# Layer norm sums of a four-layer transformer block: values and squares side by side in one TensorE matmul

## The chip, the cores and the metric

The kernel runs on one core of one Trainium2 chip. The metric is the device time of one execution in microseconds (us); the number given for a kernel is the median of several executions. The engines are named as in the profile: PE is TensorE (PEld its weight loads), DVE is VectorE, ACT is ScalarE, POOL is GpSimd, SP is SyncE, whose queue issues the DMAs.

## The reference

Four layers work on 256 latent tokens and 256 context tokens of 1024 features. Each layer is a token mixer (three kinds of attention) and a gated feed-forward network (FFN), and each of the two is followed by a layer norm. In the last layer only the latent tokens are carried on. What matters here is the norm:

```python
def layer_norm(t, g, b):
    tf = t.astype(jnp.float32)
    mu = jnp.mean(tf, axis=-1, keepdims=True)
    var = jnp.mean(jnp.square(tf - mu), axis=-1, keepdims=True)
    y = (tf - mu) * lax.rsqrt(var + LN_EPS)
    return (y * g + b).astype(t.dtype)
...
x = layer_norm(DEEPNORM_ALPHA * x + g1 * y, ln_g[i, 0], ln_b[i, 0])
f = swiglu(modulate(x, sh2, sc2), w_ffn_gate[i], w_ffn_up[i], w_ffn_down[i])
x = layer_norm(DEEPNORM_ALPHA * x + g2 * f, ln_g[i, 1], ln_b[i, 1])
```

The same two lines hold for the context tokens in layers 0 to 2. That makes 3 x 4 + 2 = 14 norms of 256 tokens each.

## The kernel before

**Layout.** Activations lie with features on the 128 partitions and tokens along the free axis. The residual stream is eight tiles `X[c]`, c = 0 to 7 (a "chunk" of 128 features each), 128 x 512 in fp32; columns 0 to 255 are the latent tokens (stream 0), 256 to 511 the context tokens (stream 1). Large products are three fp32r matmuls each (high x high, high x low, low x high), so every weight tile is loaded (`raw`), rounded by ACT (`whi`) and its rest taken by DVE or POOL (`wlo`).

**The order of work.** The kernel doesn't issue instructions as it goes. It notes them in a `Planner`, which knows the dependences and a cost for every instruction, makes 16 list schedules, keeps the one with the shortest modelled span and issues in that order. So each engine has one fixed queue, and any edit that changes a cost, a dependence or a number of buffers gives a new order everywhere. The planner's charge for a plain fp32 matmul goes by its columns: 0.083 us up to 64 columns, 0.06 us up to 128 (method `cost`). All noted instructions have the one source line L165, so the profile is read by tile names.

**The norm.** `close()` runs the last projection before a norm: for each chunk a group of matmuls (`half`, or both streams together), then `resid` (DVE adds the PSUM tile to the chunk: "DVE x") and `Norm.add(c)`. With two streams, stream 1 gets its last four chunks first, so that its norm runs while PE still has stream 0 to do; the norm of stream 0 runs under the next projections. In the last layer there is one stream, and after the last chunk PE has nothing else to do until the norm is through.

`Norm.add(c)` has ACT square the chunk (`sq`, four buffers). Chunks 0 to 6 are summed by POOL, values into `zs` and squares into the first `sq` tile, two adds of 128 x 256 for each chunk from 1 on: 12 in a norm. Chunk 7 isn't added by POOL; `REST = 1` is the number of such chunks.

`Norm.sums()` sums over the partitions by matmul with a 128 x 32 tile `ones` (filled with 1/1024). The 256 tokens go to four column groups of the array, 64 tokens each (j = 0 to 3), so that the result lies in PSUM as four blocks of 32 partitions with the means in columns 0 to 63 and the mean squares in columns 64 to 127. There are four groups of four matmuls, each matmul of 64 columns: POOL's `zs`, then chunk 7 itself (`x`), then POOL's `sq`, then chunk 7's `sq`. In the profile a plain fp32 matmul stands as two records, so one group is x8. Then follow, one behind the other, ACT and DVE instructions on 128 x 64 tiles (`v`, `R`, `Rh`, `Rl`), the matmuls with `sel` that spread the result over all partitions (`spread`, in the last norm `spread_apart`), and `apply`, two DVE instructions for each chunk, with ACT and POOL making the next `hh` and `hl`.

**The ring.** Most activation tiles come from one ring of `NSLOT = 46` slots of 2 KB per partition (tag "act"); the planner hands a slot on when the last use of its tile has ended. Some DMAs load into this ring (`rawa` in layer 0, `bias` in layer 1).

Of the kernel before, what the change touches and what calls it, by code (L numbers as in the profile page):

```python
# [12 lines left out]
F32 = mybir.dt.float32  # L13
F32R = mybir.dt.float32r
BF16 = mybir.dt.bfloat16
AF = mybir.ActivationFunctionType
# [3 lines left out]
P = 128  # L20
D = 1024
DC = D // P
T = 512
NL = 256
DEPTH = 4
# [5 lines left out]
END = (0, 1, 2, 3)  # L31
AHEAD = 0
REST = 1
NSLOT = 46
NPAIR = 6
NRAW = 4
LOOK = 2
# [4 lines left out]
LAT = slice(0, NL)  # L42
CTX = slice(NL, T)
SS = (LAT, CTX)
# [367 lines left out]
def block_kernel(ctx: ExitStack, tc: tile.TileContext, a: dict, out: bass.AP):  # L412
    nc = tc.nc
# [28 lines left out]
    nc = plan  # L442
# [65 lines left out]
            loaded[0] += 1  # L508
        return ahead.pop(key)

    X = [const.tile([P, T], F32, name=f"x{c}") for c in range(DC)]
    lng = const.tile([P, DEPTH, 2, DC], F32, name="lng")
    lnb = const.tile([P, DEPTH, 2, DC], F32, name="lnb")
    gq = const.tile([P, 3], F32, name="gq")
# [69 lines left out]

    def mod_split(hh, hl, c, s, S, B, lo_eng):
        ts = SS[s]
        xc = X[c][:, ts]
        h32 = sm.tile([P, NL], F32, tag="h32", name="h32", bufs=4)
        nc.scalar.activation(hh[c][:, ts], xc, AF.Identity, bias=B, scale=S)
        if c % 2 == 0:  # L590
            nc.scalar.activation(h32, xc, AF.Identity, bias=B, scale=S)
        else:
            nc.vector.tensor_scalar(h32, xc, S, B, op0=ALU.mult, op1=ALU.add)
        lo_eng.tensor_sub(hl[c][:, ts], h32, f(hh[c][:, ts]))
# [6 lines left out]
    class Norm:  # L601


        def __init__(self, s, l, k):
            self.s, self.n, self.zl, self.ql = s, 0, [], []
            self.g, self.b = lng[:, l, k], lnb[:, l, k]
            self.v = sm.tile([P, 3, 64], F32, tag="v", name="v", bufs=3)
            nc.scalar.activation(self.v[:, 2, 0:1], latest[0], AF.Sqrt, scale=0.0)

        def add(self, c):  # L610
            z = X[c][:, SS[self.s]]
            sq = sm.tile([P, NL], F32, tag="sq", name="sq", bufs=4)
            nc.scalar.activation(sq, z, AF.Square)
            self.n += 1
            if self.n == 1:
                self.z, self.q = z, sq
            elif self.n == 2:
                z2 = sm.tile([P, NL], F32, tag="zs", name="zs", bufs=3)
                nc.gpsimd.tensor_add(z2, self.z, z)
                nc.gpsimd.tensor_add(sq, self.q, sq)  # L620
                self.z, self.q = z2, sq
            elif self.n <= DC - REST:
                nc.gpsimd.tensor_add(self.z, self.z, z)
                nc.gpsimd.tensor_add(self.q, self.q, sq)
            else:
                self.zl.append(z)
                self.ql.append(sq)

        def sums(self):
            ps = psum("tp")  # L630
            for k, ts in enumerate(([self.z] + self.zl, [self.q] + self.ql)):
                for i, t in enumerate(ts):
                    for j in range(4):
                        nc.tensor.matmul(ps[32 * j:32 * j + 32, 64 * k:64 * k + 64], ones, t[:, 64 * j:64 * j + 64],
                                         start=i == 0, stop=i == REST)
            R = sm.tile([P, 2, 64], F32, tag="R", name="R", bufs=2)
            v = self.v
            nc.scalar.activation(v[:, 0], ps[:, 0:64], AF.Square)
            nc.vector.tensor_sub(v[:, 1], ps[:, 64:128], v[:, 0])
            nc.vector.tensor_scalar(v[:, 1], v[:, 1], 0.0, LN_EPS / ALPHA ** 2, op0=ALU.max, op1=ALU.add)  # L640
            nc.scalar.activation(v[:, 2], v[:, 1], AF.Sqrt)
            nc.vector.reciprocal(R[:, 0], v[:, 2])
            nc.vector.tensor_mul(R[:, 1], ps[:, 0:64], R[:, 0])
            rh = sm.tile([P, 2, 64], F32R, tag="Rh", name="Rh", bufs=2)
            self.R = sm.tile([P, 2, 64], F32R, tag="Rl", name="Rl", bufs=2)
            nc.vector.tensor_copy(rh, R)
            nc.vector.scalar_tensor_tensor(self.R, f(rh), neg, R, op0=ALU.mult, op1=ALU.add)
# [12 lines left out]

        def apply(self, c, h=None):
            s = self.s
            z = X[c][:, SS[s]]
            nc.vector.tensor_mul(z, z, self.bc[:, 0])
            nc.vector.tensor_sub(z, z, self.bc[:, 1])
            if h is not None:
                hh, hl, S, B = h
                mod_split(hh, hl, c, s, S[:, c, s:s + 1], B[:, c, s:s + 1], nc.gpsimd)

        def affine(self, c):  # L670
            z = X[c][:, SS[self.s]]
            nc.scalar.activation(z, z, AF.Identity, scale=self.g[:, c:c + 1], bias=self.b[:, c:c + 1])

        def steps(self, h, norms):
# [10 lines left out]
            return [self.sums, self.spread] + [lambda c=c: two(c) for c in range(0, DC, 2)]  # L685

    def resid(ps, c, s, G):
        z = X[c][:, SS[s]]
        nc.vector.scalar_tensor_tensor(z, ps, G[:, c, s:s + 1], z, op0=ALU.mult, op1=ALU.add)

    def close(load, mm, G, norms, streams, h):
# [760 lines left out]
    def begin(q):  # L1452
        c0 = 2 * q
        for c in (c0, c0 + 1):
            nc.sync.dma_start(X[c], a["x"][:, c, :])
        yield from ada_first(m, q)
        nc.vector.tensor_scalar(S0[:, c0:c0 + 2, :], m[:, 8 + c0:10 + c0, :], 1.0, None, op0=ALU.add)
        for c in (c0, c0 + 1):
# [10 lines left out]
    for l in range(DEPTH):  # L1469
# [26 lines left out]
        if last:  # L1496
# [4 lines left out]
            norms[0].spread_apart()  # L1501
            fin = norms[0]
            for c in range(DC):
                z = X[c][:, LAT]
                w = sm.tile([P, NL], F32, tag="h32", name="h32", bufs=4)
                nc.scalar.activation(w, fin.bc[1][:, :NL], AF.Identity, scale=ng[:, c:c + 1], bias=fin.b[:, c:c + 1])
                nc.vector.scalar_tensor_tensor(z, z, fin.g[:, c:c + 1], fin.bc[0][:, :NL], op0=ALU.mult, op1=ALU.mult)
# [117 lines left out]
```

## Time and profile before

| | |
|---|---|
| median of 3 executions | 2066.43 us (2065.88 to 2066.45) |
| the profiled execution, its own time | 2066.53 us |
| span of that execution in the trace | 2064.7 us |
| PE busy | 2027.8 us (98% of the span) |
| DVE, ACT, POOL busy | 1477.5, 955.9, 416.4 us (72%, 46%, 20%) |
| mean granted TensorE clock | 0.993 |

The span runs from the first to the last instruction that the profile shows; the profiled execution took 1.8 us more than its span. PE is busy nearly all the time, so a change counts where PE does less, or where PE waits for something. The profile has one row for instructions of one kind that follow each other; times are us from the start of the span, "idle before" names what ended the engine's wait.

### The profile page before, as it was taken

Reading aid. Unit: us, or ns where it says so; the run is one execution under the profiler, and the core shown is the slowest. Engines: PE = TensorE matmul, PEld = TensorE weight load, DVE = VectorE, ACT = ScalarE, POOL = GpSimd, SP = SyncE. Lnnn points to the kernel's source line nnn. Section 1 sums busy time; section 2 is a strip of 40 time slices with the busy share of each in tenths; the row PEclk is TensorE's granted clock in tenths of the full one; section 3 lists DMA queues with packets and bytes.
Section 4 is the critical chain, followed back from the end, with each engine's and each line's share of the span. In section 5 each row is a group of like instructions: output and inputs, shape, how many; then the busy total and the mean of one; then the engine's idle time right before and its main releaser. Section 6 shows DMA issues by size and latency. Waiting matters only on the chain.

```text
span 2064.7 us, 31918 instructions
## 1 busy us (share of the span) xinstructions
PE 2027.8 (98%) x12048; PEld 1758.4 (85%) x12048; DVE 1477.5 (72%) x2549; ACT 955.9 (46%) x1684; POOL 416.4 (20%) x508
## 2 busy tenths in 40 slices
PE   8999999999999999999999999999999999989997
PEld 5779988888898888988888898898888888789997
DVE  4797978796487776888785376668877845985564
ACT  4564622223387674722222386745222234766443
POOL 0345200000343334300000342251000005441002
PEclk9999999999999999999999999999999999999998
DMA  9524466665222212466564131126555642234552
GB/s 362 196 67 143 162 196 214 192 216 173 88 85 85 82 62 93 149 198 203 173 203 156 55 103 52 42 83 197 192 197 180 203 132 74 93 123 144 186 192 72
DMA packets 92120, 300.17 MB, mean 145 GB/s; under 512 B 11328, under 2 KB 11456, under 8 KB 91968
## 3 DMA queue, kind: packets, MB, share of 16 engines
q1 hardware_dynamic: 91968, 298.14, 44.5%
q8 instruction: 95, 1.56, 0.3%
q14 instruction: 57, 0.47, 0.1%
HBM read 297.05 MB, written 1.05 MB: 144 GB/s over the span
## 4 chain that ended last, share of the span: by engine, by line
PE 91%; DVE 4%; ACT 2%; issue 1%; DMA 1%; POOL 0%; SPq 0%; DVEq 0%; ACTq 0%; POOLq 0%
PE ps L165 91%; DVE wlo L165 1%; DVE nm L165 1%; ACT stk L165 1%; DVE stl L165 1%; DVE x L165 0%; ACT p L165 0%; DVE ptl L165 0%; ACT whi L165 0%; DMA bada<-in_b_ada 0%; DMA rawa<-in_w_ada 0%; DVE ps L165 0%; DVE stk L165 0%; POOL sq L165 0%; ACT x L165 0%
## 5 line engine op out<-in xcount | busy, mean ns | idle before, releaser
L165 ACT ACTIVATE whi<-raw 128x1024 fp32r<-128x1024 f32 (+3 forms) x371 | 380.1, 1028 | 757.9 <-PE ps L165 441.5
L165 PE MATMUL ps<-hh,whi 128*128 128x512 f32 (+1 forms) x1648 | 578.8, 354 | 1.7 <-ACT hh L165 1.7
L165 PE MATMUL ps<-hh,wlo 128*128 128x512 f32 (+1 forms) x1648 | 580.3, 353 | 0.0
L165 PE MATMUL ps<-hl,whi 128*128 128x512 f32 (+1 forms) x1648 | 579.9, 353 | 0.3 <-POOL hl L165 0.3
L165 DVE TENSOR_TENSOR wlo<-raw,whi 128x1024 fp32r<-128x1024 f32 (+3 forms) x359 | 439.5, 1227 | 119.2 <-ACT whi L165 117.4
L165 DVE SCALAR_TENSOR_TENSOR junk<-raw,sil 128x1024 bf16<-128x1024 f32 x320 | 392.4, 1226 | 101.3 <-DMA raw<-in_w_ada 98.6
L165 PEld LDWEIGHTS ps<-hh,wlo 128*128 128x128 f32 x1648 | 312.3, 190 | 42.2
L165 PEld LDWEIGHTS ps<-hl,whi 128*128 128x128 f32 x1648 | 312.4, 190 | 41.5 <-POOL hl L165 0.5
L165 PEld LDWEIGHTS ps<-hh,whi 128*128 128x128 f32 x1648 | 310.9, 190 | 42.1 <-ACT hh L165 1.9
L165 PE MATMUL ps<-gh,wlo 128*128 128x512 f32 (+1 forms) x800 | 271.9, 341 | 0.0
L165 PE MATMUL ps<-gh,whi 128*128 128x512 f32 (+1 forms) x800 | 271.5, 340 | 0.0
L165 PE MATMUL ps<-gl,whi 128*128 128x512 f32 (+1 forms) x800 | 271.5, 340 | 0.0
L165 DVE SCALAR_TENSOR_TENSOR x<-ps,G,x 128x256 f32<-128x256 f32 x224 | 101.8, 479 | 118.7 <-PE ps L165 118.5
L165 POOL TENSOR_TENSOR zs<-x,x 128x256 f32<-128x256 f32 x14 | 14.0, 1001 | 846.0 <-DVE x L165 846.0
L165 PEld LDWEIGHTS ps<-gl,whi 128*128 128x128 f32 x800 | 151.5, 190 | 17.1
L165 PEld LDWEIGHTS ps<-gh,wlo 128*128 128x128 f32 x800 | 151.5, 190 | 17.0
L165 PEld LDWEIGHTS ps<-gh,whi 128*128 128x128 f32 x800 | 151.6, 190 | 16.9
L165 POOL TENSOR_SCALAR p<-p,r 128x512 f32<-128x512 f32 (+1 forms) x144 | 98.9, 693 | 253.2 <-DVE r L165 232.7
L165 PE MATMUL ps<-whi,hh 128*128 128x512 f32 (+3 forms) x352 | 122.7, 350 | 1.8 <-ACT hh L165 1.8
L165 PE MATMUL ps<-wlo,hh 128*128 128x512 f32 (+3 forms) x352 | 120.7, 344 | 0.0
L165 PE MATMUL ps<-whi,hl 128*128 128x512 f32 (+3 forms) x352 | 117.8, 343 | 0.0
L165 PE MATMUL ps<-oh,wlo 128*128 128x256 f32 (+1 forms) x352 | 109.3, 316 | 0.0
(205 smaller groups left out, 3089.3 us busy)
## 6 DMA issues: line engine op xcount, KB each, us to landing
raw<-in_w_gu SPq DMA_DIRECT2D x176, 512.0 KB, 4.1
raw<-in_w_ada SPq DMA_DIRECT2D x160, 512.0 KB, 4.0
raw<-in_w_d SPq DMA_DIRECT2D x64, 448.0 KB, 4.0
rawa<-in_w_ada SPq DMA_DIRECT2D x64, 256.0 KB, 5.6
raw<-in_w_d SPq DMA_DIRECT2D x32, 512.0 KB, 3.6
raw<-in_a_qkv SPq DMA_DIRECT2D x24, 512.0 KB, 4.4
raw<-in_a_wo SPq DMA_DIRECT2D x16, 512.0 KB, 3.5
raw<-in_b_qk SPq DMA_DIRECT2D x16, 512.0 KB, 3.3
```

Of the source, the lines that this page charges most:

```text
L165: op.fn = lambda: getattr(getattr(self.nc, queue), method)(*p, **k)
```

## The change

In `sums()` the values and the squares of a group are now one moving operand of 2 x 64 columns. For this they must lie in one tile: the running sums in a new tile `zq` (128 x 2 x 256, two buffers, in place of `zs`), chunk 7 and its square in a new constant tile `end` (both streams, 128 x 2 x 2 x 256), of which the values' half takes the place of `X[7]` in all code (`xs(c, s)`). The two groups `zq` and `end` are four matmuls of 128 columns each: 8 matmuls of 128 columns where 16 of 64 columns stood. In the last layer one chunk more isn't added by POOL (`rest` is 2 there): chunk 6 and its square go to the array as two groups of 64 columns between the other two, and 10 POOL adds stand where 12 stood. The sums, squares and everything behind `sums()` are as before. The ring has 45 slots.

```diff
-NSLOT = 46
+NSLOT = 45
...
-    X = [const.tile([P, T], F32, name=f"x{c}") for c in range(DC)]
+    X = [const.tile([P, T], F32, name=f"x{c}") for c in range(DC - 1)]
+    end = const.tile([P, 2, 2, NL], F32, name="end")
+
+    def xs(c, s):
+
+        return X[c][:, SS[s]] if c < DC - 1 else end[:, s, 0]
...
         def __init__(self, s, l, k):
-            self.s, self.n, self.zl, self.ql = s, 0, [], []
+            self.s, self.rest, self.single = s, REST + (l == DEPTH - 1), []
...
         def add(self, c):
-            z = X[c][:, SS[self.s]]
+            z = xs(c, self.s)
+            if c == DC - 1:
+                nc.scalar.activation(end[:, self.s, 1], z, AF.Square)
+                return
+            if c == 0:
+                self.zq = sm.tile([P, 2, NL], F32, tag="zq", name="zq", bufs=2)
+                nc.scalar.activation(self.zq[:, 1], z, AF.Square)
+                return
             sq = sm.tile([P, NL], F32, tag="sq", name="sq", bufs=4)
             nc.scalar.activation(sq, z, AF.Square)
-            self.n += 1
-            if self.n == 1:
-                self.z, self.q = z, sq
-            elif self.n == 2:
-                z2 = sm.tile([P, NL], F32, tag="zs", name="zs", bufs=3)
-                nc.gpsimd.tensor_add(z2, self.z, z)
-                nc.gpsimd.tensor_add(sq, self.q, sq)
-                self.z, self.q = z2, sq
-            elif self.n <= DC - REST:
-                nc.gpsimd.tensor_add(self.z, self.z, z)
-                nc.gpsimd.tensor_add(self.q, self.q, sq)
-            else:
-                self.zl.append(z)
-                self.ql.append(sq)
+            if c >= DC - self.rest:
+                self.single.append((z, sq))
+                return
+            nc.gpsimd.tensor_add(self.zq[:, 0], xs(0, self.s) if c == 1 else self.zq[:, 0], z)
+            nc.gpsimd.tensor_add(self.zq[:, 1], self.zq[:, 1], sq)
 
         def sums(self):
             ps = psum("tp")
-            for k, ts in enumerate(([self.z] + self.zl, [self.q] + self.ql)):
-                for i, t in enumerate(ts):
-                    for j in range(4):
-                        nc.tensor.matmul(ps[32 * j:32 * j + 32, 64 * k:64 * k + 64], ones, t[:, 64 * j:64 * j + 64],
-                                         start=i == 0, stop=i == REST)
+            both = [self.zq, end[:, self.s]]
+            for i, t in enumerate(both):
+                if i == 1:
+                    for k, x in [(k, x) for zq in self.single for k, x in enumerate(zq)]:
+                        for j in range(4):
+                            nc.tensor.matmul(ps[32 * j:32 * j + 32, 64 * k:64 * k + 64], ones, x[:, 64 * j:64 * j + 64],
+                                             start=False, stop=False)
+                for j in range(4):
+                    nc.tensor.matmul(ps[32 * j:32 * j + 32, 0:P].rearrange("p (k t) -> p k t", k=2), ones,
+                                     t[:, :, 64 * j:64 * j + 64], start=i == 0, stop=i == 1)
...
-            nc.sync.dma_start(X[c], a["x"][:, c, :])
+            nc.sync.dma_start(X[c] if c < DC - 1 else end[:, :, 0], a["x"][:, c, :])
```

All other lines of the diff put `xs(c, s)` where `X[c][:, SS[s]]` stood.

## Rows read from the trace of the kernel before

**Rows 1.** The page's part 1, TensorE: busy us, share, instructions
```profile
PE 2027.8 (98%) x12048; PEld 1758.4 (85%) x12048; DVE 1477.5 (72%) x2549; ACT 955.9 (46%) x1684; POOL 416.4 (20%) x508
```
**Rows 2.** PE's waits, 20 to 1790 us, first and last of nine: us, times, longest
```profile
PE ps L165 <- ACT p L165: 1.7, 5, 0.5
...
PE ps L165 <- ACT oh L165: 0.2, 1, 0.2
```
**Rows 3.** Timeline of PE, a norm of layer 0: start us, us, instruction xrecords
```profile
560.93 0.28 PE L165 MATMUL ps<-gl,whi 128*128 128x256 f32 x1
...
561.39 0.41 PE L165 MATMUL ps<-sq,ones 128*32 128x64 f32 x16
...
561.95 0.28 PE L165 MATMUL ps<-gh,whi 128*128 128x256 f32 x1
562.07 0.28 PE L165 MATMUL ps<-gl,whi 128*128 128x256 f32 x1
```
**Rows 4.** Timeline of PE, the first norm, whose sums stand in two blocks
```profile
196.27 0.28 PE L165 MATMUL ps<-ol,whi 128*128 128x256 f32 x1
196.48 0.32 PE L165 MATMUL ps<-zs,ones 128*32 128x64 f32 x8
...
197.06 0.28 PE L165 MATMUL ps<-oh,whi 128*128 128x256 f32 x1
...
197.75 0.43 PE L165 MATMUL ps<-sq,ones 128*32 128x64 f32 x16
```
**Rows 5.** Timeline of PE, layer 0: 32-column weights, 128 moving columns, two blocks
```profile
23.74 0.64 PE L165 MATMUL ps<-rawa,condp 128*32 128x128 f32 x16
...
30.93 0.86 PE L165 MATMUL ps<-rawa,condp 128*32 128x128 f32 x24
```
**Rows 6.** Timeline of POOL, first norm of the last layer
```profile
1845.09 0.74 POOL L165 TENSOR_TENSOR zs<-zs,x 128x256 f32<-128x256 f32 x1 [3.34 <-DVE x L165]
...
1848.19 1.71 POOL L165 TENSOR_TENSOR sq<-sq 128x256 f32<-128x256 f32 x1
...
1850.55 1.70 POOL L165 TENSOR_TENSOR sq<-sq 128x256 f32<-128x256 f32 x1
```
**Rows 7.** Timeline of PE, the same norm
```profile
1849.42 0.28 PE L165 MATMUL ps<-oh,wlo 128*128 128x256 f32 x1
1850.64 0.32 PE L165 MATMUL ps<-zs,ones 128*32 128x64 f32 x8 [0.94 <-POOL zs L165]
...
1852.31 0.43 PE L165 MATMUL ps<-sq,ones 128*32 128x64 f32 x16 [1.23 <-POOL sq L165]
```
**Rows 8.** Timeline of ACT, the same norm
```profile
1849.80 0.94 ACT L165 ACTIVATE sq<-x 128x256 f32<-128x256 f32 x2 [0.44 <-DVE x L165]
1850.64 1.04 ACT L165 ACTIVATE whi<-raw 128x1024 fp32r<-128x1024 f32 x1
1852.80 0.22 ACT L165 ACTIVATE v<-ps 128x64 f32<-128x64 f32 x1 [1.12 <-PE ps L165]
```
**Rows 9.** Timeline of DVE, the same norm
```profile
1850.14 3.19 DVE L165 TENSOR_TENSOR wlo<-raw,whi 128x1024 fp32r<-128x1024 f32 x2
1853.26 0.21 DVE L165 TENSOR_TENSOR v<-ps,v 128x64 f32<-128x64 f32 x1
```
**Rows 10.** Stretches behind this norm: busy us by engine, PEclk (granted clock), DMA
```profile
1858.50:1862.50 4.00, 4.00 (x18) 3.95 (x19) 3.93 (x12) 3.63 (x8) 3.10 (x5) 0.50 0.01 4
1863.00:1867.00 4.00, 4.00 (x35) 4.00 (x34) 1.17 (x4) 2.58 (x5) 2.41 (x4) 1.00 0.00 0
```
**Rows 11.** Timeline of all engines, the last norm of the program
```profile
2050.92 0.73 POOL L165 TENSOR_TENSOR sq<-sq 128x256 f32<-128x256 f32 x1
...
2051.38 0.42 ACT L165 ACTIVATE sq<-x 128x256 f32<-128x256 f32 x1 [0.78 <-DVE x L165]
...
2051.70 0.46 PE L165 MATMUL ps<-sq,ones 128*32 128x64 f32 x16
```
**Rows 12.** PE's waits in the whole span, DMA alone: us, times, longest
```profile
PE ps L165 <- DMA rawa<-in_w_ada: 6.5, 5, 4.0
```

More of the change, by code (lines that the diff above doesn't have):

```diff
@@ L586, in mod_split @@
         ts = SS[s]
-        xc = X[c][:, ts]
+        xc = xs(c, s)
         h32 = sm.tile([P, NL], F32, tag="h32", name="h32", bufs=4)
@@ L662, in apply @@
             s = self.s
-            z = X[c][:, SS[s]]
+            z = xs(c, s)
             nc.vector.tensor_mul(z, z, self.bc[:, 0])
@@ L670, in affine @@
         def affine(self, c):
-            z = X[c][:, SS[self.s]]
+            z = xs(c, self.s)
             nc.scalar.activation(z, z, AF.Identity, scale=self.g[:, c:c + 1], bias=self.b[:, c:c + 1])
@@ L687, in resid @@
     def resid(ps, c, s, G):
-        z = X[c][:, SS[s]]
+        z = xs(c, s)
         nc.vector.scalar_tensor_tensor(z, ps, G[:, c, s:s + 1], z, op0=ALU.mult, op1=ALU.add)
@@ L1503, in block_kernel @@
             for c in range(DC):
-                z = X[c][:, LAT]
+                z = xs(c, 0)
                 w = sm.tile([P, NL], F32, tag="h32", name="h32", bufs=4)
```

## The prediction

> **What bounds the kernel now.** I read the page's first part, then PE's waits, then the timelines around the norms. PE is busy for 2027.8 of 2064.7 us [rows 1]. Between 20 and 1790 us, which holds twelve of the fourteen norms, PE waits for others 6.8 us in all (nine rows, from 1.7 us to 0.2 us), and none of the nine names a sum or a POOL add of a norm [rows 2]. So the twelve norms with two streams cost exactly what their instructions take on PE: POOL's adds, ACT's squares and the 3 us of small instructions behind the sums lie under other matmuls. The two norms of the last layer are different: there PE stands still until the norm is through, so that every link of the chain is paid in full [rows 7, 11]. I therefore cost the twelve by PE's time alone and the two by their chains.
>
> **Twelve norms: what one block of sums costs PE.** In layer 0 the last ordinary matmul before the sums starts at 560.93, the second one after them at 561.95, 1.02 us later; ordinary ones start 0.12 us apart, so two of these steps are 0.24 and the sums cost 0.78 us [rows 3]. How much of this is columns? Sixteen records of 64 columns (two groups of four matmuls, two records a matmul) take 0.43 us and eight take 0.32 [rows 4]: eight more records are 0.11 us, one set of four is 0.055. With 128 columns sixteen records take 0.64 and twenty-four 0.86 [rows 5]: eight more are 0.22, one set is 0.11. A set of four takes twice the time for twice the columns. Before there are 8 sets of 0.055 in a norm, 0.44 us; after it 4 sets of 0.11, 0.44 us. The rest of the 0.78 us, some 0.34, is the turn into 32-column weights and back, and there is one in either version. I take a gain of 0.0 us for each of the twelve. Bounds: if the last set's end counts longer, +0.1 us a norm; if the cost hangs on the number of records, see the rival below.
>
> By the Trainium skill, TensorEngine Tiling (Array Packing), section "Instruction Overhead", each matmul has about 60 cycles of overhead, and one of 1 column takes as long as one of 60. By that, half as many matmuls would be worth something even with equal columns. The rows here speak against it for this shape: eight records more cost 0.11 us at 64 columns, 14 ns each, less than those 60 cycles; the four column groups run beside each other.
>
> What can change is the number of turns. The first norm has its sums in two blocks: one of them takes 0.79 us from the last matmul before it to the second after it (196.27 to 197.06), so 0.55 us net; two make 1.11 against 0.78 for one block, 0.33 us more [rows 4]. Two of the twelve are split now. After the change there are two groups instead of four, and a split can only lie between `zq` and `end`. Mended, the two give back 0.7 us; with all twelve split it costs ten times 0.33, 3.3 us. The order on PE hangs on when POOL's last add and ACT's last square end, and that stays as it is, so I take 0.0.
>
> **First norm of the last layer.** PE's last matmul of the projection starts at 1849.42. ACT squares chunks 6 and 7 until 1850.74 [rows 8], but the sums end at 1852.74, because POOL is adding chunk 6: its last add runs 1850.55 to 1852.25, 1.70 us, where an undisturbed one takes 0.74 [rows 6]; DVE works through two weight tiles at that time [rows 9]. With chunk 6 summed on PE, the last add is chunk 5's, which ends at 1849.90 now [rows 6], so the last sums wait for ACT's square at 1850.74 instead: they start at about 1850.79 and end, two sets of 128 columns later, at about 1851.2. That is 1.5 us earlier than 1852.74. What is late next: ACT turns to a weight tile at 1850.64 for 1.04 us, until 1851.68, and only then can it take `v` [rows 8]; DVE has its second weight tile in hand until 1853.33, and `v` on DVE starts behind it at 1853.26 (the two overlap in the rows) [rows 9]. If DVE's queue keeps both weight tiles ahead of `v`, the gain is what faster weight tiles give without POOL beside them: some 0.3 us. If `v` comes behind the first of them, ACT's 1851.68 sets the time: ACT's `v` 0.22 us to 1851.9, DVE's at about 2.1 instead of 3.3, a gain of 1.2. If ACT's tile is put back too, 1.5. I take 1.2, since the order is made anew and DVE's `v` would be free of its sums before DVE could begin the second tile; that tile then has to fit into DVE's idle time while PE spreads the result. I keep 0.3 and 1.5 as ends. The ten POOL adds in place of twelve cost nothing else; chunk 6's two groups of 64 columns (4 sets, 0.22 us) are done while PE waits for ACT's square.
>
> Behind this norm PE runs at the lower of its two clock levels: granted 0.50 in 1858.5 to 1862.5 and 1.00 from 1863 on [rows 10]. Eighteen instructions stand in the 4 us at 0.50 and thirty-five in the next 4 us. A start 1.2 us earlier may keep the 4.4 us of slow matmuls, or shorten or lengthen them. From these rows: if the rise stays at the same moment, 1.2 us more of slow matmuls are worth half, and 0.6 of the gain is lost; if there were none at all, 4.4 us become 2.3 and 2.1 more are won. I take 0.
>
> **Last norm of the program.** Here two things end together: POOL's last add at 2051.65 and ACT's last square at 2051.80 [rows 11]. Taking POOL's add away leaves ACT's square, so nothing is won. What follows the square is one set pair of 64 columns now (the last of the sixteen records) and one of 128 after: 0.11 us more. Everything else of the sums is done while PE waits. I take +0.1, with ends of -0.2 (PE's chunks a little better ordered) and +0.5 (the resids of chunks 6 and 7 end on each other and DVE, 0.48 us each, delays one).
>
> **The small edits.** `zq` and `end` hold what `zs`, the first `sq` and `X[7]` held, with the same writers; ACT squares chunk 7 in place. The squares are as many as before. One more `sq` buffer is free during a norm, which helps only ACT and POOL, under PE. Chunk 7's load is in two pieces; it comes with the first projections. The ring of 45 is costed as a rival.
>
> **The sum.** 12 x 0.0 - 1.2 + 0.1 = -1.1 us. Against the profiled execution that is 2066.53 - 1.1 = 2065.4; the median of the runs is 0.1 lower, 2066.43, so I say 2065.3 us. A measurement of this kernel can tell about 0.2%, 4.1 us, from no change; the forecast is a quarter of that.
>
> **The rivals.**
> *A price for each record* (faster). If PE's 0.78 us a norm went by records, half would be won: 12 x 0.39 = 4.7, with the 1.1 of the last layer 5.8: 2060.6 us. For it: the turns are a large part and are not explained by the rows. Against: 0.055 and 0.11 a set [rows 4, 5]. This is also what the skill's page named above would do here. Chance 0.07.
> *A better order in the middle* (faster). The planner charges 0.083 us for each of 16 matmuls, 1.33 us a norm, where the rows show 0.78; after the change it charges 0.48. A new order arises everywhere. If it halves the 6.8 us of waits [rows 2] and the clock returns 1 us sooner: 1.1 + 3.4 + 1.0 = 5.5, 2060.9 us. Against: those waits belong to the attention of each layer, not to norms. Chance 0.12.
> *Nothing moves* (within). DVE's two weight tiles stay ahead of `v`: -0.3 + 0.1, 2066.2 us. For it: they stand so now [rows 9]. Chance 0.13.
> *Split blocks* (within, at its upper end). Ten more norms in two blocks, +3.3 - 1.1: 2068.6 us. Chance 0.08.
> *A slot too few* (slower). The loads into the ring (`bias`, `rawa`) are issued by SP in order, with weight tiles queued behind them. With one slot less a load waits for one tile more to be released, and PE feels it from the point where the weights behind it land after PE wants them. Price by the nearest row: PE waited 6.5 us in 5 waits for `rawa`, 1.3 us each [rows 12]; five more such waits are 6.5: 2071.8 us. Against: beyond 20 us PE waits for no load at all [rows 2], so there is slack. Chance 0.08; it's also the place for a new order that is worse in the attention.
> *The forecast*: 0.52, from 2064.0 (-1.5, -0.2 and 0.7 of mended splits) to 2067.8 (-0.3, +0.5 and 0.1 for each of twelve norms).
>
> **How the numbers follow.** Faster by over 0.2% (below 2062.3) are the first two rivals and a little of the forecast with the clock's 2.1: 0.21. Slower by over 0.2% (above 2070.6) is the slot and a part of the splits on top of a worse order: 0.11. Within: 0.68. The range of 8 in 10 leaves the far side of both ends out: 2061.3 to 2069.0.
>
> **What would show it right or wrong.** A block of sums in the middle still costs some 0.78 us with 16 records instead of 32. In the last layer's first norm POOL's last add ends before ACT's square, the sums end 1.5 us sooner after the last matmul, `v` on DVE some 1.2 us sooner. In the last norm, sums to end is as long as now, within 0.2 us. PE's waits between 20 and 1790 us add up to 5 to 9 us. It would be wrong if blocks shrink to 0.4 us, if PE's total wait in the middle moves by over 3 us, or if a load appears among PE's waits after 20 us.

## The result, and the profile after

The changed kernel takes 2076.91 us (median of 4 executions, 2075.44 to 2077.22) where the kernel before takes 2066.15 beside it: a ratio of 1.0053, 95% interval 1.0041 to 1.0065. It is slower by 10.8 us. The prediction, 2065.3 with a range of 2061.3 to 2069.0, was wrong in sign and in size. The profiled execution took 2077.07 us, its span is 2075.3; before, the span is 2064.7. All differences below are between spans, unless medians are named.

TensorE's line of the page's first part, as in [rows 1], and first, sixth and last of PE's nine waits from 20 to 1800 us (nearly the same stretch of the program, which is 8 us later there), as in [rows 2] (us in all, times, longest):

```profile
PE 2034.3 (98%) x11856; PEld 1758.8 (85%) x11856; DVE 1471.3 (71%) x2549; ACT 955.5 (46%) x1686; POOL 411.7 (20%) x504
```

```profile
PE ps L165 <- ACT p L165: 6.1, 6, 2.2
...
PE ps L165 <- POOL zq L165: 0.3, 1, 0.3
...
PE ps L165 <- ACT pth L165: 0.2, 1, 0.2
```

There are 192 matmul records fewer, as the diff says, and PE is busy for 6.5 us *more*. The nine waits add up to 9.5 us where they were 6.8, and a norm (`zq`) has come in among them.

To see where the 10.6 us lie I cut the span at the ends of the `resid` instructions (DVE's `x<-ps,G` and `end<-ps,G`) that close an attention or an FFN, two streams in layers 0 to 2, one in layer 3:

| stage | L0 att. | L0 FFN | L1 att. | L1 FFN | L2 att. | L2 FFN | L3 att. | L3 FFN | tail |
|---|---|---|---|---|---|---|---|---|---|
| before, us | 207.98 | 363.72 | 257.85 | 364.57 | 185.97 | 364.10 | 106.04 | 201.06 | 13.46 |
| after, us | 212.52 | 366.20 | 256.67 | 364.80 | 187.37 | 364.33 | 108.77 | 201.07 | 13.60 |
| difference | +4.54 | +2.48 | -1.18 | +0.23 | +1.40 | +0.23 | +2.73 | +0.01 | +0.14 |

The same in the view of stretches, for the two stages of layer 0 (us, PE's busy time, granted clock, DMA share, GB/s). Of the kernel after:

```profile
0.00:212.52 212.52, 197.27 (x1302) 0.99 0.54 187
212.52:578.72 366.20, 365.88 (x1822) 1.00 0.56 178
```

Of the kernel before:

```profile
0.00:207.98 207.98, 195.63 (x1317) 1.00 0.54 191
207.98:571.70 363.72, 363.72 (x1848) 1.00 0.56 178
```

In layer 0's attention most of the loss is PE standing still (15.25 us idle for 12.35) and a little clock; in layer 0's FFN PE is busy for 2.2 us more. Those are two different causes. Over the whole span the three ways to lose time come out as: PE idle +4.1 us (41.0 for 36.9); half of PE's busy time in the stretches that show a granted clock of 0.50, +1.8 (8.9 for 7.1); the rest, work at the full clock, +4.7. Of this last, 4.2 us is in the sums themselves, as follows.

**The sums.** A block of a norm now, in the timeline of PE (start, us, instruction), to set beside [rows 3]:

```profile
200.75 0.28 PE L165 MATMUL ps<-ol,whi 128*128 128x256 f32 x1
200.96 0.43 PE L165 MATMUL ps<-zq,ones 128*32 128x128 f32 x8
201.20 0.40 PE L165 MATMUL ps<-end,ones 128*32 128x128 f32 x8
201.53 0.39 PE L165 MATMUL ps<-oh,wlo 128*128 128x256 f32 x1
201.75 0.28 PE L165 MATMUL ps<-oh,whi 128*128 128x256 f32 x1
```

From 200.75 to 201.75, less two steps of 0.12, is 0.76 us; it was 0.78 with 32 records. The other norm of the same layer, that of stream 0, looks like this:

```profile
210.69 0.28 PE L165 MATMUL ps<-oh,wlo 128*128 128x256 f32 x1
210.90 0.41 PE L165 MATMUL ps<-zq,ones 128*32 128x128 f32 x2
211.24 0.39 PE L165 MATMUL ps<-hh,whi 128*128 128x256 f32 x1
211.55 0.41 PE L165 MATMUL ps<-zq,ones 128*32 128x128 f32 x2
211.89 0.62 PE L165 MATMUL ps<-hh,whi 128*128 128x256 f32 x3
212.44 0.41 PE L165 MATMUL ps<-zq,ones 128*32 128x128 f32 x4
212.78 0.39 PE L165 MATMUL ps<-hl,whi 128*128 128x256 f32 x1
213.01 0.28 PE L165 MATMUL ps<-hh,wlo 128*128 128x256 f32 x1
...
215.15 0.28 PE L165 MATMUL ps<-hh,wlo 128*128 128x256 f32 x1
215.36 0.42 PE L165 MATMUL ps<-end,ones 128*32 128x128 f32 x8
215.72 0.38 PE L165 MATMUL ps<-hh,whi 128*128 128x256 f32 x1
215.94 0.28 PE L165 MATMUL ps<-hl,whi 128*128 128x256 f32 x1
```

The group of `zq` is itself cut: column group j = 0 alone, j = 1 alone, j = 2 and 3 together, and `end` a fourth piece behind other work. 210.69 to 213.01 is 2.32 us with six steps of ordinary matmuls in it (0.72), so 1.60; 215.15 to 215.94 is 0.79, less 0.24 is 0.55. Together 2.15 us, 1.4 more than in one block. Three norms stand so in four pieces (layer 0's two and layer 1's first, all of stream 0), two more in two pieces (1387 and 1390 us, 1752 and 1754 us). Summed over the twelve norms in this way, with 0.12 us for every ordinary matmul and leaving waits out, the sums take 10.5 us before and 14.7 us after.

**Layer 0's attention.** ACT's timeline before, around the first softmax instruction `p` and the table load (ACT_TABLE_LOAD, which stands where ACT goes over to another function) ahead of it, followed by PE's matmul that waits for `p`:

```profile
89.46 1.28 ACT L165 ACT_TABLE_LOAD   x1
91.01 0.47 ACT L165 ACTIVATE p<-ps,nm 128x256 f32<-128x256 f32 x1 [0.27 <-DVE nm L165]
...
92.08 0.50 PE L165 MATMUL ps<-kh,qh 128*128 128x512 f32 x1 [0.45 <-ACT p L165]
```

and after:

```profile
91.43 1.28 ACT L165 ACT_TABLE_LOAD   x1 [1.61 <-DVE nm L165]
92.72 0.47 ACT L165 ACTIVATE p<-ps,nm 128x256 f32<-128x256 f32 x1
...
93.80 0.50 PE L165 MATMUL ps<-kh,qh 128*128 128x512 f32 x1 [2.22 <-ACT p L165]
```

Before, the 1.28 us of the load run while ACT waits for `nm`; after, the load itself comes behind that wait, `p` is late and PE stands for 2.22 us (0.45 before). Behind it PE's clock drops. Stretches of the kernel after (us; busy us of PE, PEld, DVE, ACT, POOL; granted clock; DMA share; GB/s):

```profile
95.30:98.60 3.30, 3.30 (x9) 2.60 (x8) 1.56 (x3) 0.62 (x2) 0.69 (x2) 0.50 0.00 0
98.70:102.00 3.30, 3.30 (x17) 2.21 (x15) 0.00 (x0) 0.30 (x1) 0.00 (x0) 1.00 0.23 80
```

Nine matmul records in 3.3 us at 0.50 (1.2 GHz), seventeen in the next 3.3 at 2.4 GHz. The kernel before has no such stretch there. Two later waits for `p`, of 1.42 us (153.37) and 1.01 us (158.31), come on top.

**The first norm of the last layer.** PE, POOL, ACT and DVE, to set beside [rows 6 to 9]:

```profile
1859.81 0.28 PE L165 MATMUL ps<-oh,wlo 128*128 128x256 f32 x1
1861.26 0.42 PE L165 MATMUL ps<-end,ones 128*32 128x128 f32 x8
1858.22 1.73 POOL L165 TENSOR_TENSOR zq<-zq,sq 128x256 f32<-128x256 f32 x1
1862.05 0.20 ACT L165 ACTIVATE v<-ps 128x64 f32<-128x64 f32 x1
1862.18 1.22 DVE L165 TENSOR_TENSOR wlo<-raw,whi 128x1024 fp32r<-128x1024 f32 x1 [0.33 <-ACT whi L165]
1863.32 0.22 DVE L165 TENSOR_TENSOR v<-ps,v 128x64 f32<-128x64 f32 x1
```

From PE's last projection matmul: the sums end 1.87 us later (3.32 before), ACT's `v` starts 2.24 later (3.38 before), DVE's `v` 3.51 later (3.84 before). DVE still takes its second weight tile ahead of `v`. The FFN's first matmul, with `hh`, starts 8.85 us behind the last projection matmul (8.96 before) and its sixtieth 18.19 behind it (18.18): the stretch at 0.50 that follows is 10.24 us long in both kernels and starts 0.3 us later here (3.5 us behind that matmul, 3.2 before), so PE's clock rises later too. The last norm of the program:

```profile
2060.88 0.28 PE L165 MATMUL ps<-gh,wlo 128*128 128x256 f32 x1
2062.97 0.22 DVE L165 TENSOR_TENSOR v<-ps,v 128x64 f32<-128x64 f32 x1 [1.25 <-ACT v L165]
```

2.09 us from the last matmul to DVE's `v`; before it is 2.01 (2050.48 to 2052.49).

### The profile page after: what moved, and what is told of

Read it like the earlier page. It is cut to its first block, busy times and chain, and to the rows that moved or that the text cites. A ratio compares the mean times of both kernels' runs of the same rounds, so it can differ in the third digit from the quotient of the medians.

```text
span 2075.3 us, 31555 instructions
## 1 busy us (share of the span) xinstructions
PE 2034.3 (98%) x11856; PEld 1758.8 (85%) x11856; DVE 1471.3 (71%) x2549; ACT 955.5 (46%) x1686; POOL 411.7 (20%) x504
## 4 chain that ended last, share of the span: by engine, by line
PE 91%; DVE 4%; ACT 3%; issue 1%; DMA 1%; POOL 0%; SPq 0%; DVEq 0%; ACTq 0%; POOLq 0%
PE ps L165 91%; DVE nm L165 1%; ACT p L165 1%; ACT stk L165 1%; DVE ptl L165 0%; DVE wlo L165 0%; DVE stl L165 0%; ACT whi L165 0%; DMA bada<-in_b_ada 0%; DMA rawa<-in_w_ada 0%; ACT L165 0%; DVE junk L165 0%; ACT pth L165 0%; DVE x L165 0%; ACT x L165 0%
## 5 line engine op out<-in xcount | busy, mean ns | idle before, releaser
L165 POOL TENSOR_TENSOR zq<-x,x 128x256 f32<-128x256 f32 x14 | 13.0, 931 | 837.2 <-DVE x L165 837.2
L165 DVE SCALAR_TENSOR_TENSOR x<-ps,G,x 128x256 f32<-128x256 f32 x196 | 88.8, 477 | 115.9 <-PE ps L165 115.8
L165 ACT ACTIVATE p<-ps,nm 128x512 f32<-128x512 f32 (+1 forms) x144 | 84.6, 591 | 50.6 <-DVE nm L165 42.7
```

The costliest lines, as they stand in the source:

```text
L165: op.fn = lambda: getattr(getattr(self.nc, queue), method)(*p, **k)
```

## The experiments

Two theories stand against each other at the start. **Order**: the changed sizes (ring of 45, other charges, other tiles) make the planner take another list, and that list is worse in the attention and cuts the sums up; the new form of the sums costs nothing. **Form**: the sums with values and squares side by side are themselves dearer, or the ring of 45 is too small. Every kernel was timed beside the kernel before (medians 2066.45, 2066.22 and 2066.36 us for the three groups e1 to e4, e5 to e8, e9 to e12). "List" is which of its 16 schedules the planner kept; that follows from the planner's code, without a chip. "Blocks" counts the stretches of sums in PE's trace.

| | list | median us | ratio, 95% | blocks | L0 att. | L3 att. |
|---|---|---|---|---|---|---|
| before | 12 | 2066.15 | | 16 | 207.98 | 106.04 |
| after | 15 | 2076.91 | 1.0053 [1.0041, 1.0065] | 25 | 212.52 | 108.77 |
| e1 before, ring 45 | 7 | 2064.37 | 0.9992 [0.9983, 1.0002] | 21 | 206.60 | 105.62 |
| e2 after, sums together | 15 | 2071.37 | 1.0025 [1.0015, 1.0036] | 14 | 212.39 | 105.91 |
| e3 after, ring 46 | 13 | 2067.28 | 1.0005 [0.9995, 1.0015] | 19 | 206.52 | 107.61 |
| e4 last chunk alone | 12 | 2066.51 | 1.0001 [0.9991, 1.0010] | 16 | 207.23 | 106.11 |
| e5 before, ring 45 | 15 | 2069.27 | 1.0015 [1.0006, 1.0024] | 15 | 211.42 | 106.22 |
| e6 = e2 | 7 | 2069.86 | 1.0019 [1.0009, 1.0028] | 14 | 207.23 | 109.29 |
| e7 = after | 7 | 2074.24 | 1.0037 [1.0023, 1.0051] | 21 | 207.62 | 109.98 |
| e8 after, old charge | 13 | 2070.50 | 1.0022 [1.0013, 1.0031] | 14 | 210.67 | 107.27 |
| e9 new form alone | 12 | 2068.61 | 1.0012 [1.0003, 1.0022] | 14 | 207.85 | 105.98 |
| e10 = e4, tile on POOL | 12 | 2067.21 | 1.0004 [0.9994, 1.0013] | 16 | 207.45 | 104.85 |
| e11 = e2, ring 46 | 11 | 2068.44 | 1.0011 [1.0002, 1.0020] | 14 | 208.36 | 107.09 |
| e12 = e10, ring 45 | 7 | 2064.69 | 0.9994 [0.9985, 1.0003] | 21 | 206.68 | 105.70 |

**e1. The ring of 45 alone, old form.**

```diff
-NSLOT = 46
+NSLOT = 45
```

> The kernel before with one edit, NSLOT 46 to 45. Theory 1 (a new order is what costs: ring and charges only cause it): PE busy changes only by its turns into and out of the sums, and the time moves by the PE idle time of the attention stages; layer 0 up to its first norm gains or loses, anything from -1 to +5 us, with no PE wait on a load beyond the first 20 us; whole kernel 2064 to 2071. Rival A (the missing slot itself: loads or tiles wait for it): +4 us or more in layer 0's attention, PE idle there +2.5 or more as in the changed kernel, whole kernel 2070 or more. Rival B (the matmul of two groups side by side is dearer on PE): 2066, no change, for the form is the old one.

2064.37 us: not slower, and its interval still holds 1. So 45 slots are enough. Its twenty-one blocks cost some: the sums of the twelve norms take 12.4 us for 10.5 in the kernel before, a split 0.3 to 0.4 us, and none of its norms is in more than two pieces. The time is no longer for it, since other stages gain more. Most splits lie between groups; but in two norms one matmul of `zs` stands alone, so that a group can be cut up in the old form too, with the old charge:

```profile
825.19 0.30 PE L165 MATMUL ps<-zs,ones 128*32 128x64 f32 x2
```

**e2. The changed kernel, all sums in one block.** Every matmul of `zq` and `end` gets a dependence on the square of chunk 7, so that none can start alone.

```diff
                nc.scalar.activation(end[:, self.s, 1], z, AF.Square)
+                self.closing = plan.ops[-1]
...
+                    plan.ops[-1].deps.add(self.closing)
```

> The changed kernel, with the planner told that zq's matmuls depend on ACT's square of chunk 7 as end's do, so that the groups of a norm can't be issued apart. Theory 1: one block of sums in each norm; the stage behind layer 0's first norms loses its +2.2 us of PE time and the split norms of layers 1 and 2 theirs, PE busy falls by 4 to 6 us to about 2029, whole kernel 2070 to 2073 if layer 0's attention stays as in the changed kernel (+4.5), 2066 if that order happens to be mended as well. Rival A: the +4.5 in layer 0's attention stays, since the ring is as small. Rival B: a block of 16 records costs more than the 0.78 us of before, PE busy stays above 2032, whole kernel above 2074.

2071.37 us, 5.5 us less than the changed kernel. The norm that stood in four pieces, in PE's timeline:

```profile
215.00 0.42 PE L165 MATMUL ps<-zq,ones 128*32 128x128 f32 x8
215.24 0.40 PE L165 MATMUL ps<-end,ones 128*32 128x128 f32 x8
```

The sums of the twelve norms take 9.7 us here for 14.7, five less, and layer 0's FFN is back at 363.97 us. The agreement of 5.0 with 5.5 isn't exact by stage: two stretches of 3.4 us at 0.50 (788 and 1802 us in the kernel after) are gone as well, and other work is up by 2.2. Layer 0's attention stays at 212.39, so that its loss has nothing to do with the sums.

**e3. The changed kernel with 46 slots** (and three `sq` tiles, which makes room for the slot).

```diff
-NSLOT = 45
+NSLOT = 46
...
-            sq = sm.tile([P, NL], F32, tag="sq", name="sq", bufs=4)
+            sq = sm.tile([P, NL], F32, tag="sq", name="sq", bufs=3)
```

> The changed kernel with NSLOT 46 again, and three buffers for sq instead of four to make room. Theory 1: another order again; layer 0's attention may gain or lose by a few us, splits of sums stay (PE busy 2031 to 2034); whole kernel 2068 to 2077. Rival A (the slot itself): layer 0's attention comes back by 3 to 4.5 us, PE idle there to about 12.4 us, whole kernel 2071 to 2073. Rival B: PE busy stays at 2034, no change, 2077.

2067.28 us, not to be told from the kernel before. The whole new computation is in it; what differs, but for the slot and the `sq` tile, is the list that the planner took. Its split norms have two pieces, none four.

**e4. The old form with one chunk more on TensorE in the last layer.**

```diff
+            self.rest = REST + (l == DEPTH - 1)
...
-            elif self.n <= DC - REST:
+            elif self.n <= DC - self.rest:
...
-                                         start=i == 0, stop=i == REST)
+                                         start=i == 0, stop=i == self.rest)
```

> The kernel before, and in the last layer chunk 6 is summed by TensorE, in the old form of four groups; ring 46. Its order can differ only where the last layer's two norms reach. Theory 1: all stages up to layer 3's last projection stay within 0.3 us; the first norm of the last layer gains the 0.3 to 1.5 us of my prediction, the last norm -0.2 to +0.5; whole kernel 2065 to 2066. Rival A and B: the same here. Rival C (this chunk is itself part of the loss: the sums of chunk 6 come before the last matmuls and delay chunk 7): the last layer's FFN stage is not shorter or is longer, whole kernel 2066 to 2067.

2066.51 us: nothing. It keeps the order of before up to layer 3, and it shows the same chain as the changed kernel: `v` on DVE 3.51 us behind the last matmul, the sixtieth FFN matmul 18.15 behind it. So the second part of the change, alone, is worth nothing that can be measured. Its profile also gives the size of what is not order (the profiled execution, 2064.37 us, is the shortest of its ten): in layer 1's attention, with the same queue on PE, it is 1.44 us shorter than the kernel before. The stretch of before, and that of e4 a little earlier in its own time:

```profile
781.00:784.00 3.00, 3.00 (x9) 2.27 (x8) 2.84 (x7) 2.69 (x6) 1.38 (x2) 0.50 0.14 57
```

```profile
779.00:782.00 3.00, 2.21 (x11) 1.77 (x12) 2.61 (x7) 2.76 (x7) 1.07 (x2) 1.00 0.49 165
```

A stretch at 0.50 of 3.4 us comes or stays out under one and the same order. Differences of single stages below some 1.5 us in one profile are therefore not read as effects.

**e5. The kernel before, ring of 45, made to take its own 15th list, as the changed kernel did.**

```diff
-            if best is None or span < best[0]:
+            if n == 14:
```

> The kernel before (old form of the sums, old charges) with ring 45, and the planner made to take its 15th pass instead of the one of shortest modelled span (the 7th in e1). The changed kernel and e2 take their 15th. Theory 1 (layer 0's +4.5 us is the order of the pass that was taken, and has nothing to do with the norms): layer 0 up to the last resid of its attention takes 212 to 213 us with PE idle 15 to 15.7, as in the changed kernel, though no norm is changed; PE waits of about 2.2, 1.4 and 1.0 us for p near 94, 153 and 158 us stand there; whole kernel 2067 to 2073. Rival (the new form or zq and end in SBUF slow layer 0): 206 to 208 us as in e1 and before.

2069.27 us. No line of the norm is changed, and layer 0's attention takes 211.42 us (e1, the same kernel with list 7: 206.60). The same wait stands at the same place:

```profile
91.31 1.28 ACT L165 ACT_TABLE_LOAD   x1 [1.61 <-DVE nm L165]
...
93.68 0.50 PE L165 MATMUL ps<-kh,qh 128*128 128x512 f32 x1 [2.23 <-ACT p L165]
```

This settles most of the first 4.5 us: 3.4 of them stand in a kernel whose sums are untouched, and the two lists of this one kernel (e1, e5) differ by 4.8 us in that stage. Up to 180 us e5 and the changed kernel have the same instructions in the same order on PE and DVE, and PE's in e5 start 0.10 to 0.14 us sooner all the way from 30 us on, but for the 4 us around the stretch at the lower clock, which begins at 94.09 us there for 95.24. PE's longest wait between 60 and 165 us goes with the list and the ring, whatever the form of the sums: 2.22, 2.22 and 2.23 us with list 15 and 45 slots (after, e2, e5), 2.12 us with list 7 and 45 slots (e1, e6, e7, e12), 0.74 to 0.75 us with list 12 and 46 slots (before, e4, e9, e10).

**e6 and e7. The counterproof**: the kernel of e2 and the changed kernel, both with list 7 (`if n == 6:`).

> e2 (the changed kernel with each norm's sums kept in one block) with the 7th pass taken, the one that e1 took with the same ring. Theory 1: layer 0's attention falls from 212.4 to 206.6 us, the blocks stay one a norm, PE busy 2026 to 2029; whole kernel 2063 to 2067, equal to the kernel before. Rival: layer 0's attention stays at 212 since the new tiles are there; whole kernel 2070 to 2072.

> The changed kernel with nothing but the 7th pass taken. Theory 1: layer 0's attention 206.6 us; seven norms' worth of extra turns stay (21 blocks of sums instead of 14, one norm in four pieces), PE busy 2029 to 2032; whole kernel 2067 to 2072, between e6 and the changed kernel. Rival: 2075 to 2077.

Layer 0's attention is good in both, 207.23 and 207.62 us. Yet e7 still takes 2074.24 us and e6 2069.86: 4.4 us for 21 blocks against 14. In the profiles the sums take 2.6 us more in e7 and PE is idle for 1.3 us more. And list 7 is no good list for them: in layer 3's attention they lose 3.3 and 3.9 us against the kernel before. PE's waits there, e6 from 1750 to 1850 us:

```profile
PE ps L165 <- ACT p L165: 4.4, 2, 2.6
```

The kernel before has one such wait there, of 2.6 us. So "take another list" doesn't mend the changed kernel; each list pays in another attention.

**e8. The changed kernel with the old charge for its sums.** In the kernel after the planner charges 0.06 us for a matmul of 128 columns, 0.48 us a norm; here it is twice 0.083.

```diff
+            if n == P and len(out.shape) == 3:
+                return 0.166
```

> The changed kernel with the planner's charge for a sums matmul of 2 x 64 columns set to 0.166 us instead of 0.06, so that 8 of them are charged as the 16 of before were. Theory 1: the sums stand in one block in each norm (14 blocks), PE busy 2026 to 2029; the order in the attention is another one again, layer 0 anything from 206 to 213; whole kernel 2063 to 2071. Rival (the splits come from the two groups being ready at different times, whatever the charge): 20 or more blocks, PE busy 2031 or more.

14 blocks, 2070.50 us: 6.4 less than the changed kernel. With the dearer matmul no group of this form is broken up, here and in e9, and the split goes away without a dependence; that isn't so for every form and list, as e1 shows. (It also takes another list, the 13th, which loses 2.7 us in layer 0's attention.)

**e9. The new form alone**, one chunk in the last layer as before, with 46 slots, the old charge and list 12, the one that the kernel before has.

```diff
-            self.s, self.rest, self.single = s, REST + (l == DEPTH - 1), []
+            self.s, self.rest, self.single = s, REST, []
```

> The new form of the sums alone: values and squares side by side, old charge for it (0.166 us a matmul), ring 46 with three sq buffers, no extra chunk in the last layer, and the 12th pass taken, as the kernel before does; so layer 0's attention has the order of before. Theory 1 (the form itself is worth nothing on PE, the order is what costs): one block of sums a norm at 0.77 us, PE busy 2025 to 2028, layer 0's attention 206.5 to 208, whole kernel 2064 to 2069 with what the other attention stages do. Rival B (the form is dear): PE busy 2031 or more and 2072 or more. Rival (a price for each record): PE busy 5 us lower than before, 2061.

2068.61 us, 2.2 above the kernel before. Up to layer 2 the stages of the profiled execution (2069.82 us) agree within 0.6 us but for layer 1's attention (+1.39). There PE's order isn't that of before, and the stretch at 0.50 that before has (1.7 us) is missing: PE stands still for 0.9 us more and works 2.2 us more at the full clock, which no run took apart. In the last layer +1.07 us lie in the stage of the FFN, where the form does cost something, since both POOL adds of chunk 6 now stand ahead of any sum:

```profile
1854.29 0.66 PE L167 MATMUL ps<-zq,ones 128*32 128x128 f32 x8 [3.46 <-POOL zq L167]
```

In the old form the values' group could go before the squares' add had ended [rows 7]. The changed kernel, which has chunk 6 on TensorE there, has no such wait: the two parts of the change belong together.

**e10. Freeing DVE.** e10 is e4 with the low part of DVE's second weight tile made by POOL, so that `v` has nothing ahead of it.

```diff
+POOL_SPLIT |= {u_key(DEPTH - 1, 2, 1)}
```

> e4 (the kernel before with chunk 6 summed by TensorE in the last layer), and one weight tile's low part, the one that DVE made ahead of v in the last layer's first norm, made by POOL instead. My theory on where the last layer's gain went: DVE's queue holds that tile ahead of v (v 3.5 us after the last matmul in e4, 3.8 before). With it gone, v on DVE comes 2.4 to 2.8 us after the last matmul, the FFN starts 0.7 to 1.1 us sooner than in e4; of this 0.3 to 1.1 us is left in the FFN stage's length, since PE's clock is at its lower level until it has worked for some us. Rival (POOL's tile slows DVE's small instructions as much): v soon but Rl late, no gain; whole kernel 2065.5 to 2066.5 either way.

2067.21 us. `v` on DVE does come 2.48 us behind the last matmul, 1.0 sooner than in e4, and it is lost at once (DVE and POOL of e10):

```profile
1849.80 0.23 DVE L165 TENSOR_TENSOR v<-ps,v 128x64 f32<-128x64 f32 x1 [0.44 <-ACT v L165]
1850.06 2.07 DVE L165 TENSOR_SCALAR v<-v 128x64 f32<-128x64 f32 x1
1849.73 2.34 POOL L165 TENSOR_TENSOR wlo<-raw,whi 128x1024 fp32r<-128x1024 f32 x1 [1.80 <-ACT whi L165]
```

The 64-column TENSOR_SCALAR takes 0.20 us in e4; here it ends at 1852.13, when POOL's instruction ends. The FFN starts 9.49 us behind the last projection matmul, 0.85 later than in e4.

**e11 and e12. Is there a version that beats both?** e11 is e2 with the 46 slots and the three `sq` tiles of e3 and the planner's own list; e12 is e10 with the ring of 45.

> e2 (the changed kernel, sums of a norm in one block) with ring 46 and three sq buffers, the planner taking its own best pass (its 11th). Theory 1: another order, nothing else: layer 0's attention 205 to 209 us, PE busy 2025 to 2029, whole kernel 2063 to 2070. Rival A (it is the ring's 46th slot that gives the time back): 2064 to 2067, since e3 with the same ring and five more turns had 2067.3.

> e1 (the kernel before with ring 45) with the two edits of e10. Theory: e1's order in layers 0 to 2, 2064.4, less what e10 gains over the kernel before in the last layer, 0.3 to 1.1: 2063 to 2064.3, faster than the kernel before by 0.1%. Rival: e1's small gain is not there in another set of runs, 2065.5 to 2066.5.

e11 takes 2068.44 us, so that the 46th slot alone doesn't bring back e3's time, and e12 2064.69. e1 and e12 are the two lowest, both with 45 slots, the old form and list 7; both intervals still hold 1. No version that beats the kernel before was found.

## Why the prediction was wrong

**The price of one block: right.** 0.76 us with 16 records, 0.78 with 32, as 0.44 + 0.34 in either version said. The rival with a price for each record (2060.6) is refuted by that row.

**"A split can only lie between `zq` and `end`": the step that failed.** A group is four matmuls on four column groups, and nothing binds the four. The prediction's two rows of split blocks [rows 4] were both split between groups, and I took that for the only way. Three norms came out in four pieces, 1.4 us each where a split was priced at 0.33. In all the sums cost PE 4.2 us more, for a forecast of 0.0 and a rival of +3.3 with chance 0.08. The rival's size was nearly right, its mechanism not: seven norms still stand in one block. With the new form it hangs on the planner's charge, which fell from 1.33 to 0.48 us a norm: the three kernels with the lower charge and no tie have 25, 19 and 21 blocks (after, e3, e7), and restoring the charge (e8, e9) or tying the matmuls together (e2, e6, e11) gives 14. The prediction named this charge, but only as a reason for a *better* order. The planner's own price for a turn is too low as well: 0.087 us each way (`TURN` in the code), 0.17 for two, where a split costs 0.33 in the trace [rows 4].

**"That stays as it is": the second failure.** The 0.0 rested on an unchanged order around the norms, and the only places where order was priced were a gain (2060.9, chance 0.12) and half a sentence under the slot rival. The list that came out loses 4.54 us in layer 0's attention, of which 2.9 is PE idle and 1.7 the clock behind a wait, and e5 shows the same stage at 211.42 us with the norm untouched. Kernels of the new form with one block a norm, and all but the same work to do, lie between 2068.4 and 2071.4 us here (e2, e6, e8, e9, e11), and the kernel before, with 45 slots, between its two lists at 2064.4 and 2069.3 (e1, e5). All five of the new form are above the kernel before. Where the order is the same the traces show no price of the form (e5 beside the changed kernel), and the FFN stages of layers 1 and 2 take 363.9 to 364.6 us in these five, 364.0 to 364.6 in before, e4 and e5; a small cost in the attention stages, beside that of the lists, isn't excluded. A spread of some 5 us from order alone was not in the range; its low and high ends held only the known edits. With PE waiting only 6.8 us in the middle [rows 2] there was little to win by a new order and much to lose: the same row spoke for a rival on the slow side with a larger chance than the fast one.

**Why list 15 has the table load behind the wait.** The reason isn't a place in a queue: before and after, PE has the same instructions in the same order up to 90 us, ACT and DVE up to 100. But `p` before waits for DVE's semaphore alone; after, that wait is an instruction of its own at 91.38 us, ahead of the load, and `p` waits for ACT's own semaphore besides. The addresses in the two programs show why: list 15 puts this `p` into the ring slot of a `sqh` tile, which ACT had written, list 12 into that of a `qn` tile, which DVE had. That another slot alone would bring the load back in front of the wait was not tried.

**Layer 3's attention**, +2.73 us: PE stands still for 4.9 us where it was 3.9 (among it 1.4 us for POOL's `p`, and 3.2 for ACT's where before has 2.6), a norm in two pieces is 0.6 us, and some 1.3 us more are other work of PE at the full clock; the clock's stretch of 3.4 us is in both. e6 and e7 lose still more there. It changes with the list (104.9 to 110.0 us in the runs), and that the order is its cause is argued, not shown; no run took it apart further.

**First norm of the last layer: links right, sum wrong.** POOL's add does end ahead of ACT's square, the sums end 1.45 us sooner (1.5 forecast), ACT's `v` 1.14 sooner. DVE's `v` gained 0.33 for the 1.2 that I chose between 0.3 and 1.5. The choice rested on DVE's `v` being placed ahead of the second tile; it wasn't, which is the rival "nothing moves". Where it was (e7: `v` 2.48 us behind the last matmul), the tile moved in behind `v`, and the sixtieth FFN matmul came 17.89 us behind the last projection matmul for 18.19: 0.3 of a gain of 1.0 is left. So in e7, which has the order that the prediction chose, the 1.2 isn't there either. The clock's term of 0 was right for its length (10.24 us in both) but not for its place: the stretch moved 0.3 us back with respect to the last projection matmul. Of the 0.33 us at `v`, 0.11 is left at the FFN's first matmul and nothing at its sixtieth.

**Last norm: right.** +0.08 us to `v` for +0.1.

**The slot too few: refuted.** e1 is not slower, and no load stands among PE's waits after 20 us.

**What the prediction named as signs.** "PE's waits 5 to 9 us": 9.5. "Wrong if PE's total wait in the middle moves by over 3 us": 2.7, just short of it, while 6.5 of the 10.6 us came through PE's busy time. The sign for that, a block at 0.78 us, held for the blocks that stand whole; none asked how many blocks there would be.

## What to carry to other kernels

Where a planner makes the order, an edit that changes a charge, a buffer count or a tile is also a throw of the order: price it as a term of its own, from the spread of lists that the planner itself can give, and let it reach further to the slow side the fuller PE already is. A set of small matmuls on separate column groups is cheap only while it is issued together; tie it together, or charge it so that nothing is gained by breaking it up (the higher charge did that here for the new form, not for the old; a higher charge for the turn was not tried). When a chain on the critical path is shortened, look first at what else stands in the queue of the next engine: what is won ahead of an engine with a 1.2-us tile in hand is lost there.

## What the runs showed of the hardware

- One column group of 32 (two records of 128 columns) among ordinary matmuls costs about as much as all four: three pieces (one, one and two groups, from 210.90 on) take 1.60 us, 0.53 each, and a piece with all four 0.55 (215.15 to 215.94 less 0.24). So most of a block's cost doesn't hang on how many column groups are in it; by the 0.11 us for a set of four records [rows 5] the columns are an estimated 0.22 of the 0.55 us, and the rest is put down here to the turn into the 32-column weights and back.
- An ACT_TABLE_LOAD of 1.28 us was free ahead of ACT's wait for `nm` (89.46 us, before) and paid in full behind it (91.43 us, after); PE's wait is 0.45 or 2.22 us.
- A TENSOR_SCALAR of DVE on 128x64 took 2.07 us instead of 0.20 beside a POOL instruction of 2.34 us that had begun 0.33 us earlier, and ended with it. The Trainium skill, SBUF — State Buffer, section "Who interferes with whom", says that `tensor_scalar` may use the port pair that DVE shares with GpSimd, and that the engine that comes second waits for the other's whole instruction; the trace of e10 agrees, with 1852.13 against 1852.07 for the two ends.
- A stretch of 3.4 us at the lower clock in the middle of the attention came in one profile and stayed out of another with the same queue on PE (before and e4), and is worth 1.4 to 1.7 us.
